# Dilated attention in a two-layer hybrid block: tokens of one residue side by side, heads paired on halves of the array, outputs with features on partitions

## Chip, cores, metric

One core of a Trainium2 chip runs the whole program. The metric is the time of one execution in microseconds, the median of several runs; a profiled execution of its own shows where the time goes. TensorE (PE) multiplies, VectorE (DVE), ScalarE (ACT) and GpSimd (POOL) do the rest, SyncE (SP) issues most DMAs.

## What is computed

512 tokens of width 1024 pass two layers. Each layer has a mixer with three branches (retention, gated delta rule, dilated attention), cross attention to 256 memory tokens, and a convolutional gated MLP, all in float32. The change concerns the third branch and, in the order of its products, the first. Dilated attention, shortened:

```python
DIL_GROUPS = ((128, 1), (512, 4), (2048, 16))     # window, dilation; 4 heads of 64 features each
q, k = partial_rope(d_q), partial_rope(d_k)       # first 16 features of a head are rotated
for gi, (window, dilation) in enumerate(DIL_GROUPS):
    # tokens of one residue modulo dilation form a sequence; blocks of window // dilation,
    # each sees itself and the block before it, at a distance of at most window // dilation
    o_g, lse_g = dilated_window_attention(q[:, :, gi], k[:, :, gi], v[:, :, gi], dilation, window // dilation)
wts = softmax(stack(lses), axis=groups)
o_dil = sum(wts * stack(outs)).reshape(B, T, 256)
merged = gate0 * (o_ret @ w_br_ret) + gate1 * (o_gdn @ w_br_gdn) + gate2 * (o_dil @ w_br_dil)
```

## The kernel before

Activations stand with features on partitions and the 512 tokens along the free axis. Projections are computed from a high and a low part of each operand (fp32r): three matmuls a tile (`mm3`, L214 to L216) into one of four accumulators of PSUM pool `pd`. Weights come in slabs of 512 KB over SP, and ScalarE and VectorE split each into `wh` and `wl` (L203, L204) with the highest priority. The small products of the attention parts are plain fp32; each such call is two load-and-matmul pairs in the trace, a transposition is one.

The code is written as a data flow. A scheduler orders the instructions of every engine ahead of time with a simulated clock: by priority, which is the place in the program unless `soon()` or `first()` raises it, and as operands and buffers are free in that simulation. Engines then run their lists in order. PSUM pools `pa` and `pg` have two buffers each; the scratch tags `ta` three and `tg` four.

`rotated` (L346) multiplies a projection by a cosine row (L349), swaps features (L350), multiplies by sines on POOL (L351) and adds (L352). `mixer` calls it for the twelve tiles `dqk` (three groups; two tiles of queries, two of keys; two heads to a tile, on partitions 0 to 63 and 64 to 127). The projections `dqk` and the values `dv` are on TensorE while `retention` (L595) works through four heads one after another: scores `rs` (L614), state products `rS` (L619), outputs `ro` (L626) and `ri` (L630).

`dilated` (L667) has two halves, i = 0 for group 0 and i = 1 for groups 1 and 2 together. Each has four steps n of 128 queries, and in each step two turns hh, for the heads on the lower and on the upper partitions. A turn writes scores `ds` of two heads (L687; L691, where every 4th token is read by a strided slice), adds the mask, takes the maximum and the exponential, transposes the probabilities (`dt`, L705), copies them to `dp` in SBUF, and multiplies by the values (`do`, L716) with the probabilities stationary and 64 features streaming. The outputs `oA` and `oB` have tokens on partitions. After that the logarithmic sums of the two halves are exchanged through DRAM, the outputs are scaled (L745), transposed (`dA`, `dB`, L750 and L754) and added with a strided view that puts residues back into the order of tokens (L756), and split into `odil` (L757, L758).

`dilated` is followed in the program by `branch` for j = 0, 1, 2. A branch has eight pairs of a gate (24 matmuls) and an output projection `y`; only the third reads `odil`. As the gates and the first two branches need nothing of `dilated`, the scheduler fills TensorE with them while the attention's steps wait for the other engines. The triangular inverse of the second branch uses small tiles of the array: L504 multiplies partitions 0 to 31 into 0 to 31 and 64 to 95 into 64 to 95, L506 partitions 0 to 31 into 32 to 63. After the mixer, four loads of memory tokens use the tag `tg` (L1086, L1087).

Of the kernel before, what the change touches and what calls it, by code (L numbers as in the profile page):

```python
# [12 lines left out]
AF = mybir.ActivationFunctionType  # L13
# [5 lines left out]
P = 128  # L19
# [4 lines left out]
NB = 4  # L24
# [77 lines left out]
def tile_hybrid(ctx, tc, xT, memT, pos, wts, cst, kst, prm, rows, outT):  # L102
# [243 lines left out]
    def rotated(out, p, tab, swap):  # L346
        t = td("rot")
        with soon():
            V.tensor_tensor(out, p, tab[:, 0, :], ALU.mult)  # L349
            V.stream_shuffle(t, p, swap)  # L350
        G.tensor_tensor(t, t, tab[:, 1, :], ALU.mult)  # L351
        V.tensor_tensor(out, out, t, ALU.add)  # L352
# [241 lines left out]

    def retention(l, rqk, rv, dec):  # L595
# [13 lines left out]
        for h in range(H):  # L609
            j, r = h // 2, slice(64 * (h % 2), 64 * (h % 2) + 64)  # L610
            hs = slice(h * P, (h + 1) * P)
            sp = pa(f"rs{h}", (NB, P))
            for b in range(NB):
                PE.matmul(sp[:, b, :], lhsT=rqk[r, 2 + j, blk(b)], rhs=rqk[r, j, blk(b)], start=True, stop=True)  # L614
            st = ta(f"st{h}", (NB, P))
            V.tensor_tensor(st, sp, again(dec[:, h * P:(h + 1) * P], NB), ALU.mult)
            kv = pa(f"rS{h}", (NB - 1, P))
            for b in range(NB - 1):
                PE.matmul(kv[:, b, :], lhsT=ks[j][:, b, :], rhs=rv[:, b, hs], start=True, stop=True)  # L619
            state = states[j][r]  # L620
            S.activation(state[:, 0], kv[r, 0], AF.Copy)
            for b in range(1, NB - 1):
                V.tensor_tensor(state[:, b], state[:, b - 1], kv[r, b], ALU.add)
            op = pg(f"ro{h}", (NB, P))
            for b in range(NB):
                PE.matmul(op[:, b, :], lhsT=st[:, b], rhs=rv[:, b, hs], start=True, stop=True)  # L626
            S.activation(o[:, :, h, :], op, AF.Copy)
            ip = pg(f"ri{h}", (NB - 1, P))
            for b in range(1, NB):
                PE.matmul(ip[:, b - 1, :], lhsT=rqk[r, j, blk(b)], rhs=state[:, b - 1], start=True, stop=True)  # L630
            for b in range(1, NB):
                q = K_QD + 3 * h + b - 1
                V.scalar_tensor_tensor(o[:, b, h, :], ip[:, b - 1], dec[:, q:q + 1], o[:, b, h, :],
                                       ALU.mult, ALU.add)
            sq = ta(f"rsq{h}", (NB, P))
            for b in range(NB):
                i = b * H + h
                S.activation(sq[:, b, :], o[:, b, h, :], AF.Square, accum_out=ssq[:, i:i + 1])
# [28 lines left out]
    def dilated(l, dq, dk, dv0, dv12, kc):  # L667

        oA = region("q1", [NB, H, 64], f"oA{l}")
        oB = region("q2", [NB, H, 64], f"oB{l}")  # L670
        st = [small("stA", 32), small("stB", 32)]
        sd = [dp.tile([T, 8], F32, name=f"sd{l}{i}") for i in range(2)]
        masks = (kc[:, 0:256], kc[:, 256:512])
        for i, o in enumerate((oA, oB)):
            v8 = st[i].rearrange("p (n e) -> p n e", e=8)
            for n in range(NB):
                for hh in range(2):
                    w = P if i == 0 and n == 0 else 2 * P
                    nk = w // P
                    m = masks[i][:, 2 * P - w:]  # L680

                    r, hs = slice(64 * hh, 64 * hh + 64), slice(hh, H, 2)
                    pool = (pa, pg)[hh]
                    sp = pool(f"ds{i}{n}{hh}", (2, 2 * P))[:, :, :w]
                    for hp in range(2):
                        if i == 0:
                            PE.matmul(sp[:, hp, :], lhsT=dq(0, hp)[r, blk(n)],  # L687
                                      rhs=dk(0, hp)[r, (n + 1) * P - w:(n + 1) * P], start=True, stop=True)
                        else:
                            for g in (1, 2):  # L690
                                PE.matmul(sp[:, hp, (g - 1) * P:g * P], lhsT=dq(g, hp)[r, n::NB],  # L691
                                          rhs=dk(g, hp)[r, n::NB], start=True, stop=True)
# [13 lines left out]
                    pt = ta(f"dp{i}{n}{hh}", (2, nk, P))  # L706
                    S.activation(pt, tpz, AF.Copy)
                    op = pool(f"do{i}{n}{hh}", (2, 64))
                    for hp in range(2):
                        h = 2 * hp + hh  # L710
                        for k in range(nk):
                            if i == 0:
                                rhs = dv0[:, n + 1 - nk + k, h * 64:h * 64 + 64]
                            else:
                                rhs = dv12[:, n, k * 256 + h * 64:k * 256 + h * 64 + 64]
                            PE.matmul(op[:, hp, :], lhsT=pt[:, hp, k, :], rhs=rhs,  # L716
                                      start=k == 0, stop=k == nk - 1)
                    S.activation(o[:, n, hs, :], op, AF.Copy)
            if i == 0:
                G.dma_start(sd[0].rearrange("(n p) e -> p n e", p=P), v8)  # L720
            else:
# [555 lines left out]
```

## Time and profile before

| | us |
|---|---|
| median of 3 runs | 2159.71 |
| lowest, highest | 2157.39, 2163.61 |
| the profiled execution | 2165.57 |
| its span, first to last instruction | 2163.7 |
| TensorE busy | 2118.1 |
| VectorE busy | 1374.7 |
| ScalarE busy | 927.5 |
| GpSimd busy | 391.5 |

The page says how long each engine was busy and which chain of work ended last. In the timeline a row is a run of like instructions: start, length, engine, line, operation, tiles and shapes, count. Matmuls overlap, so what one costs is the distance between starts and not its length. In the table by stretch, PEclk is TensorE's granted clock as a share of full speed. The dilated stage and its filler stand at about 355 to 552 us in the first layer and at 1415 to 1612 us in the second.

### The profile page before, as it was taken

The numbers are of one execution on the slowest core, as the hardware profiler recorded it, in microseconds if no ns is written. First come the engines' busy times: TensorE is split into PE (matmuls) and PEld (weight loads), VectorE is DVE, ScalarE is ACT, GpSimd is POOL, SyncE is SP. The second block draws the span as 40 slices with busy tenths as digits, with TensorE's granted clock in tenths as the row PEclk, the third lists the DMA queues.
The fourth block names the chain that finished last, engine by engine and source line by source line (L and its number), as shares of the span: only waits on it lengthen the run. The fifth ranks groups of instructions, "written<-read, shape, count | busy, mean of one in ns | idle before, by whom it ended". The sixth has DMA issues, their size and how long they took to land.

```text
span 2163.7 us, 28806 instructions
## 1 busy us (share of the span) xinstructions
PE 2118.1 (98%) x10665; PEld 1783.8 (82%) x10665; DVE 1374.7 (64%) x2571; ACT 927.5 (43%) x1885; POOL 391.5 (18%) x403
## 2 busy tenths in 40 slices
PE   7899999999999999999999999999999999999997
PEld 6778889888888888888888788988888888888886
DVE  7995585435577786377478846743455788745754
ACT  4733334433455444244356242443343564433443
POOL 6731220002130211011121121100111302100112
PEclk9999999989999999999999999999999999999998
DMA  4233222122233223333332322321333323323322
GB/s 144 78 96 109 84 84 88 60 88 87 94 98 117 78 98 98 98 97 98 111 101 83 110 85 69 93 78 50 98 98 98 108 88 98 98 93 102 98 90 86
DMA packets 69756, 201.58 MB, mean 93 GB/s; under 512 B 18352, under 2 KB 21168, under 8 KB 69104
## 3 DMA queue, kind: packets, MB, share of 16 engines
q1 hardware_dynamic: 67120, 192.34, 28.2%
q0 software_dynamic: 2352, 7.37, 1.1%
q8 instruction: 83, 1.36, 0.3%
q14 instruction: 57, 0.47, 0.1%
q10 hardware_dynamic: 144, 0.04, 0.0%
HBM read 192.85 MB, written 6.88 MB: 92 GB/s over the span
## 4 chain that ended last, share of the span: by engine, by line
PE 86%; DVE 8%; DMA 2%; issue 1%; ACT 1%; SPq 0%; DVEq 0%; ACTq 0%
PE gate L214 4%; PE gate L215 4%; PE gate L216 4%; PE uu L214 3%; PE ua L214 3%; PE uu L215 3%; PE ua L215 3%; PE ua L216 3%; PE uu L216 3%; PE dn L214 3%; PE dn L215 3%; PE dn L216 3%; PE dqk L214 2%; PE dqk L216 2%; PE dqk L215 2%; DVE wl L204 2%
## 5 line engine op out<-in xcount | busy, mean ns | idle before, releaser
L203 ACT ACTIVATE wh<-w 128x512 fp32r<-128x512 f32 (+2 forms) x689 | 429.6, 625 | 852.0 <-PE dn L215 129.4
L204 DVE TENSOR_TENSOR wl<-w,wh 128x512 fp32r<-128x512 f32 (+2 forms) x689 | 507.8, 739 | 381.9 <-ACT wh L203 357.7
L214 PE MATMUL gate<-xgh,wh 128*128 128x512 f32 x384 | 157.3, 410 | 0.0
L215 PE MATMUL gate<-xgl,wh 128*128 128x512 f32 x384 | 155.7, 405 | 0.0
L216 PE MATMUL gate<-xgh,wl 128*128 128x512 f32 x384 | 155.1, 404 | 0.0
L216 PE MATMUL uu<-xgh,wl 128*128 128x512 f32 x320 | 124.6, 389 | 0.0
L214 PE MATMUL uu<-xgh,wh 128*128 128x512 f32 x320 | 124.6, 389 | 0.0
L215 PE MATMUL uu<-xgl,wh 128*128 128x512 f32 x320 | 124.6, 389 | 0.0
L214 PE MATMUL ua<-xgh,wh 128*128 128x512 f32 x320 | 124.6, 389 | 0.0
L216 PE MATMUL ua<-xgh,wl 128*128 128x512 f32 x320 | 124.6, 389 | 0.0
L215 PE MATMUL ua<-xgl,wh 128*128 128x512 f32 x320 | 124.6, 389 | 0.0
L214 PE MATMUL dn<-ah,wh 128*128 128x512 f32 x308 | 120.0, 390 | 0.0
L215 PE MATMUL dn<-al,wh 128*128 128x512 f32 x308 | 120.0, 389 | 0.0
L216 PE MATMUL dn<-ah,wl 128*128 128x512 f32 x308 | 116.2, 389 | 0.0
L1017 POOL TENSOR_TENSOR fya<-fya,fyu 128x512 f32<-128x512 f32 x44 | 72.9, 1657 | 223.1 <-DVE fyu L1001 221.3
L278 POOL TENSOR_TENSOR acc<-acc,sq 128x512 f32<-128x512 f32 x41 | 59.4, 1448 | 244.3 <-ACT sq L277 243.3
L778 POOL TENSOR_TENSOR mg<-mg,g 128x512 f32<-128x512 f32 x32 | 45.8, 1432 | 298.0 <-DVE g L776 298.0
L214 PEld LDWEIGHTS gate<-xgh,wh 128*128 128x128 f32 x384 | 75.4, 196 | 17.6 <-issue 2.6
L216 PEld LDWEIGHTS gate<-xgh,wl 128*128 128x128 f32 x384 | 75.0, 195 | 16.7 <-issue 0.7
L215 PEld LDWEIGHTS gate<-xgl,wh 128*128 128x128 f32 x384 | 75.2, 196 | 15.2 <-issue 0.4
L216 PE MATMUL g<-xgh,wl 128*128 128x512 f32 x192 | 77.6, 405 | 1.5 <-DVE wl L204 1.5
L351 POOL TENSOR_TENSOR rot<-rot,tab 128x512 f32<-128x512 f32 x32 | 47.0, 1478 | 173.7 <-DVE rot L350 164.1
(497 smaller groups left out, 5266.7 us busy)
## 6 DMA issues: line engine op xcount, KB each, us to landing
w<-in_wts SPq DMA_DIRECT2D x331, 512.0 KB, 3.5
tab<-tabs_d POOLq DMA_DIRECT2D x4, 512.0 KB, 4.1
mem<-in_memT POOLq DMA_DIRECT2D x8, 256.0 KB, 3.6
x<-in_xT SPq DMA_DIRECT2D x2, 1024.0 KB, 5.2
x_d<-x SPq DMA_DIRECT2D x8, 256.0 KB, 3.8
x<-x_d SPq DMA_DIRECT2D x2, 1024.0 KB, 5.4
out<-x SPq DMA_DIRECT2D x8, 256.0 KB, 2.3
w<-in_wts SPq DMA_DIRECT2D x7, 256.0 KB, 2.5
```

Of the source, the lines that this page charges most:

```text
L203: S.activation(wh[:, :m], w[:, o:o + m], AF.Copy)
L204: V.tensor_tensor(wl[:, :m], w[:, o:o + m], wh[:, :m], ALU.subtract)
L214: PE.matmul(out, lhsT=lh, rhs=rh, start=start, stop=False)
L215: PE.matmul(out, lhsT=lh, rhs=rl, start=False, stop=False)
L216: PE.matmul(out, lhsT=ll, rhs=rh, start=False, stop=stop)
L278: eng.tensor_tensor(acc, acc, sq, ALU.add)
L351: G.tensor_tensor(t, t, tab[:, 1, :], ALU.mult)
L778: G.tensor_tensor(mt, mt, g, ALU.add)
L1017: G.tensor_tensor(ya, ya, yu, ALU.mult)
```

## The change

Five edits. `rotated` can write its sum so that the tokens of one residue modulo 4 stand side by side; groups 1 and 2 use that, with a scratch tile from `ta`, and their scores then read whole blocks. A helper `together` issues a list of matmuls one right behind the other. In `retention` two heads, and in `dilated` both turns of a step, issue their products alternately on the lower and the upper half of the array's rows. The product with the values is turned round: values stationary, probabilities streaming, the two turns alternately on the left and the right half of the array's columns, so that outputs come with features on partitions. The scale of the outputs is spread over 64 features on POOL and brought to that layout by a product with the identity, and the transpositions `dA` and `dB` go.

```diff
-    def rotated(out, p, tab, swap):
+    def rotated(out, p, tab, swap, every=1):
         t = td("rot")
+        a = out if every == 1 else ta("rota")
         with soon():
-            V.tensor_tensor(out, p, tab[:, 0, :], ALU.mult)
+            V.tensor_tensor(a, p, tab[:, 0, :], ALU.mult)
             V.stream_shuffle(t, p, swap)
         G.tensor_tensor(t, t, tab[:, 1, :], ALU.mult)
-        V.tensor_tensor(out, out, t, ALU.add)
+        if every == 1:
+            V.tensor_tensor(out, a, t, ALU.add)
+        else:
+            a, t = (v.rearrange("p (t n) -> p n t", n=every) for v in (a, t))
+            V.tensor_tensor(out.rearrange("p (n t) -> p n t", n=every), a, t, ALU.add)
...
+    def together(calls):
+        for i, call in enumerate(calls):
+            with (first if i else soon)():
+                ins = call()
+                if i:
+                    tc.keep_in_program_order(ins)
...
     def retention(l, rqk, rv, dec):
...
+        for j in range(2):
+            pair = [(2 * j + e, slice(64 * e, 64 * e + 64)) for e in range(2)]
+            sps = [pa(f"rs{h}", (NB, P)) for h, r in pair]
+            def score(b, e):
+                r = pair[e][1]
+                return PE.matmul(sps[e][:, b, :], lhsT=rqk[r, 2 + j, blk(b)], rhs=rqk[r, j, blk(b)],
+                                 start=True, stop=True)
+            together([lambda a=(b, e): score(*a) for b in range(NB) for e in range(2)])
...
+            ips = [pool(f"ri{h}", (NB - 1, P)) for (h, r), pool in zip(pair, (pg, pa))]
+            def before(b, e):
+                r = pair[e][1]
+                return PE.matmul(ips[e][:, b - 1, :], lhsT=rqk[r, j, blk(b)], rhs=states[j][r][:, b - 1],
+                                 start=True, stop=True)
+            together([lambda a=(b, e): before(*a) for b in range(1, NB) for e in range(2)])
...
     def dilated(l, dq, dk, dv0, dv12, kc):
-        oA = region("q1", [NB, H, 64], f"oA{l}")
-        oB = region("q2", [NB, H, 64], f"oB{l}")
+        oA = region("q1", [2, NB, P], f"oA{l}")
+        oB = region("q2", [2, NB, P], f"oB{l}")
...
+                pools = (pa, pg)
+                sps = [pools[hh](f"ds{i}{n}{hh}", (2, 2 * P))[:, :, :w] for hh in range(2)]
+                def score(hp, g, hh):
+                    keys = slice((n + 1) * P - w, (n + 1) * P) if i == 0 else blk(n)
+                    to = slice(0, w) if i == 0 else blk(g - 1)
+                    return PE.matmul(sps[hh][:, hp, to], lhsT=dq(g, hp)[halves[hh], blk(n)],
+                                     rhs=dk(g, hp)[halves[hh], keys], start=True, stop=True)
+                together([lambda a=(hp, g, hh): score(*a)
+                          for hp in range(2) for g in ((0,), (1, 2))[i] for hh in range(2)])
...
-                                PE.matmul(sp[:, hp, (g - 1) * P:g * P], lhsT=dq(g, hp)[r, n::NB],
-                                          rhs=dk(g, hp)[r, n::NB], start=True, stop=True)
...
-                    pt = ta(f"dp{i}{n}{hh}", (2, nk, P))
-                    S.activation(pt, tpz, AF.Copy)
-                    op = pool(f"do{i}{n}{hh}", (2, 64))
...
-                            PE.matmul(op[:, hp, :], lhsT=pt[:, hp, k, :], rhs=rhs,
-                                      start=k == 0, stop=k == nk - 1)
-                    S.activation(o[:, n, hs, :], op, AF.Copy)
+                    pts.append(tg(f"dp{i}{n}{hh}", (2, nk, P)))
+                    S.activation(pts[hh], tpz, AF.Copy)
+                op = pools[n % 2](f"do{i}{n}", (2, P))
+                def values(hp, k, hh):
...
+                    return PE.matmul(op[halves[hh], hp, :], lhsT=v, rhs=pts[hh][:, hp, k, :],
+                                     start=k == 0, stop=k == nk - 1)
+                together([lambda a=(hp, k, hh): values(*a)
+                          for hp in range(2) for k in range(nk) for hh in range(2)])
+                S.activation(o[:, :, n, :], op, AF.Copy)
...
-            o16 = o.rearrange("p n h d -> p (n h) d")
-            V.tensor_tensor(o16, o16, over(a, 64), ALU.mult)
+            for hp in range(2):
+                wide = ta(f"dw{i}{hp}", (NB, 2, 64))
+                G.tensor_copy(wide, a.rearrange("p (n h o) -> p n h o", h=H, o=1)[:, :, 2 * hp:2 * hp + 2, :]
+                              .to_broadcast([P, NB, 2, 64]))
+                rows = pa(f"dr{i}{hp}", (NB, P))
+                for n in range(NB):
+                    PE.matmul(rows[:, n, :], lhsT=wide[:, n].rearrange("p h d -> p (h d)"), rhs=ident,
+                              start=True, stop=True)
+                V.tensor_tensor(o[:, hp], o[:, hp], rows, ALU.mult)
...
-            transposes(pA, lambda n: oA[:, n, hs, :].rearrange("p h d -> p (h d)"))
...
-            transposes(pB, lambda n: oB[:, n, hs, :].rearrange("p h d -> p (h d)"))
...
-                rotated(dqk[g][:, i, :], fm_one(f"dqk{g}{i}", xg), tab, SWAP8)
+                rotated(dqk[g][:, i, :], fm_one(f"dqk{g}{i}", xg), tab, SWAP8, NB if g else 1)
```

## Rows read from the trace of the kernel before

**Rows 1.** The page: busy time of the engines, and the chain that ended last.
```profile
PE 2118.1 (98%) x10665; PEld 1783.8 (82%) x10665; DVE 1374.7 (64%) x2571; ACT 927.5 (43%) x1885; POOL 391.5 (18%) x403
PE 86%; DVE 8%; DMA 2%; issue 1%; ACT 1%; SPq 0%; DVEq 0%; ACTq 0%
```
**Rows 2.** By stretch: length, busy us (instructions) per engine, PEclk, DMA share, GB/s.
```profile
355.00:420.00 65.00, 65.00 (x317) 52.35 (x315) 30.85 (x55) 28.93 (x72) 0.78 (x1) 1.00 0.22 71
420.00:500.00 80.00, 80.00 (x347) 66.64 (x346) 27.20 (x48) 28.16 (x70) 5.66 (x6) 0.89 0.25 79
1480.00:1560.00 80.00, 80.00 (x350) 66.56 (x349) 27.45 (x51) 27.74 (x70) 4.58 (x4) 0.91 0.24 80
```
**Rows 3.** Groups by line: form and count | busy us, mean ns | idle before.
```profile
L691 PE MATMUL ds<-dqk 64*128 64x128 f32 x128 | 38.7, 446 | 0.0
```
**Rows 4.** Timeline of TensorE, a step of i = 1: start, length, engine, line, form, count.
```profile
475.62 1.00 PE L716 MATMUL do<-dv,dp 128*128 128x64 f32 x8
476.55 2.24 PE L691 MATMUL ds<-dqk 64*128 64x128 f32 x8
478.72 0.72 PE L214 MATMUL gate<-xgh,wh 128*128 128x512 f32 x1
479.23 0.63 PE L215 MATMUL gate<-xgl,wh 128*128 128x512 f32 x1
```
**Rows 5.** Timeline of TensorE, part of a step of i = 0.
```profile
404.92 1.13 PE L687 MATMUL ds<-dqk 64*128 64x256 f32 x4
405.97 0.66 PE L705 MATMUL dt<-c,dm 128*128 128x128 f32 x4
406.39 0.47 PE L215 MATMUL gate<-xgl,wh 128*128 128x512 f32 x1
```
**Rows 6.** Timeline of TensorE, retention: scores alone, state products, then two heads' products meeting.
```profile
296.53 1.16 PE L614 MATMUL rs<-rqk 64*128 64x128 f32 x8
297.61 0.94 PE L619 MATMUL rS<-rv,rk 128*128 128x128 f32 x6
298.30 0.48 PE L216 MATMUL dqk<-xgh,wl 128*128 128x512 f32 x1
...
304.83 0.27 PE L630 MATMUL ri<-rst,rqk 64*128 64x128 f32 x1
304.94 0.27 PE L614 MATMUL rs<-rqk 64*128 64x128 f32 x1
304.94 0.27 PE L630 MATMUL ri<-rst,rqk 64*128 64x128 f32 x1
305.05 0.27 PE L614 MATMUL rs<-rqk 64*128 64x128 f32 x1
```
**Rows 7.** Timeline of TensorE, the triangular inverse: tiles of 32x32, then of 64x64.
```profile
197.92 0.19 PE L506 MATMUL x<-T,ys 32*32 32x32 f32 x1
197.94 0.20 PE L504 MATMUL x<-ys,T 32*32 32x32 f32 x2
197.95 0.19 PE L506 MATMUL x<-T,ys 32*32 32x32 f32 x1
...
202.39 1.14 PE L515 MATMUL y<-A 64*64 64x64 f32 x16
```
**Rows 8.** Additions on VectorE and POOL (ns min/median/max or mean); the rotation's stretch.
```profile
L352 DVE TENSOR_TENSOR dqk<-dqk,rot x24: 676/684/949, 233.2 to 1374.0; 128x512 f32<-128x512 f32 x24
L756 DVE TENSOR_TENSOR dsA<-dsA,dB x4: 1085/1100/1110, 512.7 to 1575.8; 128x512 f32<-128x512 f32 x4
L778 POOL TENSOR_TENSOR mg<-mg,g 128x512 f32<-128x512 f32 x32 | 45.8, 1432 | 298.0 <-DVE g L776 298.0
290.00:310.00 20.00, 20.00 (x112) 16.87 (x111) 19.76 (x55) 4.71 (x11) 6.11 (x4) 1.00 0.27 89
```
**Rows 9.** Timeline: the last write of the output, and its first reader on TensorE.
```profile
519.97 0.69 DVE L758 TENSOR_TENSOR odil<-dsA,odil 128x512 fp32r<-128x512 f32 x1
...
551.30 0.39 PE L214 MATMUL y<-odil,wh 128*128 128x512 f32 x1
```

## What is predicted

> **What bounds the kernel now.** The page first: TensorE is busy 98% of the span, and 86% of the chain of work that ended last is TensorE's [rows 1]. The table by stretch then shows the dilated stage of each layer without a gap: TensorE busy 65.00 of 65 us and 80.00 of 80, vector and scalar engines under half of the time [rows 2]. The gaps between the short matmuls of the attention are filled with gate and branch matmuls that need nothing from it. So a microsecond of TensorE taken out here should come out of the total, as long as such filler lasts. The same table shows the granted clock at 0.89 and 0.91 in the second half of the stage, 1.00 before it [rows 2]. Last comes the order on TensorE, from which I read spacing (start to next start, over the count): a matmul's duration includes its tail.
>
> **Strided scores (groups 1 and 2).** 64 instructions a layer write a product of 128 columns from every 4th token. Eight take 2.17 us (476.55 to 478.72), 0.271 each [rows 4]; the line's busy time gives 38.7/128 = 0.302 [rows 3]. Summing start to start over a layer's twelve groups I get 0.29: 18.6 us. The rotation now writes the tokens side by side, so they become the kind of matmul that retention has. Eight of those, all on one half of the array, take 1.08 us, 0.135 each; where two products on different halves stand together the spacing falls to 0.11 a pair, 0.055 each (304.83, 304.94, 304.94, 305.05) [rows 6]. The change alternates the halves call by call, so I take 0.055: 64 x 0.055 = 3.5, a saving of 15.1 a layer. Bounds: 0.135 (10.0 saved), 0.055.
>
> **Scores of group 0.** Twenty-four of 256 columns at 1.05/4 = 0.262 [rows 5] and eight of 128 at 0.135 [rows 6]: 7.4 us. In pairs 256 columns should take twice 0.11: 24 x 0.11 + 8 x 0.055 = 3.0. Saved 4.4; bounds 0 and 4.4.
>
> **Retention.** 56 instructions a layer on halves of the array. Their 32 groups in both layers, the first at 296.53, sum to 6.0 us a layer, because some pairs meet already [rows 6]. All alternating: 56 x 0.055 = 3.1. Saved 2.9; bounds 0 and, had none met before (56 x 0.135 = 7.6), 4.5.
>
> **Values.** Before, the stationary side is a 128x128 block of probabilities and 64 columns stream; eight take 0.93 us, 0.116 each [rows 4]; 120 a layer make 13.9 us. After, 64 columns of values are stationary, 128 columns stream, and two heads use the left and the right columns of the array. No row shows 128x64 tiles. The nearest is the triangular inverse: tiles of 32x32, of which two read the same rows and write different columns. There a step of one L506 and two L504 takes 0.03 us (197.92 to 197.95), while sixteen instructions of 64 columns on one and the same tile take 1.14 us, 0.07 each, or 0.035 for 32 columns [rows 7]: three instructions in the time of one, so tiles on the same rows do overlap. I take 0.055: 6.6 us, saved 7.3. Bounds: 0.116 (nothing saved) and 0.055.
> The Trainium skill speaks against this: "TensorE: Matmul & The Clock Gate", Part 3 ("What overlaps and what doesn't"), says that a weight load overlaps running matmuls only when the row group differs, and column halves share all row groups. By that page these loads would stand in line; by the rows above they wouldn't. It is a rival below.
>
> **Scaling by rows.** The outputs now have features on partitions, so the softmax weights are widened on POOL and brought to that layout by 32 new full-width instructions a layer; such ones take 0.69/6 = 0.115 [rows 6]: 3.7 us. Sixteen transposes go, at 0.42/4 = 0.105 [rows 5]: 1.7. Net +2.0. The four copies a layer on POOL, priced by its nearest row of the same size at 1.43 us [rows 8], run on an engine that is busy 5.66 of 80 us [rows 2], and wait in its queue only behind the branch additions; they cost nothing while the filler lasts.
>
> **Rotation.** Sixteen additions (eight a layer) now read every 4th element. An addition took 0.684, the nearest strided one 1.100 [rows 8]; +0.42 x 16 = 6.7 us of VectorE, where it is 19.76 of 20 us busy [rows 8]. TensorE doesn't wait there now, and the additions stand behind the two instructions that free the accumulator. The new scratch tile shares three buffers with retention, and VectorE could wait for one. Bounds 0 (a strided read isn't faster) and 6.7; I take 2 in all, because the excess has the following stage's idle VectorE to run into.
>
> **The clock.** After a score group of eight with the values ahead of it (475.62 to 478.72) the following matmuls take 0.63 us instead of 0.39 [rows 4, 9]: the 1.2 GHz level. After the narrower groups of the first half they don't [rows 5], and that half has 1.00 throughout [rows 2]. In both halves the short groups look alike but for the strided scores, so with them the cause should go. (1 - 0.89) x 80 + (1 - 0.91) x 80 = 16.0 us; a part lies under score groups which I have counted already, so 14. Bounds 0 and 16.
>
> **Nothing for the rest.** The probability tiles move to the four "tg" buffers, which pushes the four loads of the memory behind this stage; their readers come after the branches. Fewer, wider copies of outputs, and the products with the keys in one order, change only engines that idle. Switches: a matmul behind a short group lasts some 0.1 longer (0.47 at 406.39, 0.39 elsewhere [rows 5, 9]); fewer groups would give at most 3 us a layer back, which I leave out.
> The Trainium skill's page "TensorEngine Tiling (Array Packing)", Key Properties, says that a change of tiling mode drains the array, and the values bring one mode more. By it some 16 groups x 2 x 0.1 = 3 us would be lost over both layers; no row shows that the mode and not the short group costs the 0.1.
>
> **The sum.** A layer: -15.1 - 4.4 - 2.9 - 7.3 + 2.0 = -27.7; two: -55.4. Clock -14, rotation +2: -67.4. The profiled execution took 2165.57 us: 2098.2. The median of the runs is 5.9 below it, so 2092.
>
> **Rivals.**
> 1. The column halves don't overlap: values stay near 0.116, +7.3 x 2 = 14.6, 2106. For it: no row of this tile shape. Against: [rows 7]. Chance 0.11.
> 2. Their loads stand in line with the streams: 0.11 and half of the 0.115 of a full-width load, 0.168 each, 20.1 us instead of 6.6, +27 in all: 2119. For it: the rule of the Trainium skill named under the values. Against: [rows 7]. Chance 0.04.
> 3. The clock still falls, as the stage keeps many short matmuls: +14, 2106. Against: the first half, as dense in them, holds 1.00 [rows 2]. Chance 0.07.
> 4. The change doesn't do what it says: the calls stand alternately in the program, but the halves don't run together. Scores at 0.135 and 0.262, retention at 0.135, values at 0.116: 5.1 + 4.4 + 4.5 + 7.3 = 21.3 a layer, 2135. Against: the pairs in [rows 6], which met by chance and did. Chance 0.05.
> 5. The other side: TensorE runs out of filler, because the attention's own steps become longer. Its output is ready at 520.7, its first reader starts at 551.3, 30.6 us later [rows 9]. With some 32 us less to do TensorE gets there at about 519. Each layer has 8 steps, of now (520.7 - 355)/8 = 20.7 us. Two score groups of 2.17 become one of 0.9 in four of them, some 14 us off the chain; that is the cushion. But both halves of a step are now tied: scores need a slot in both PSUM pools, values wait for the slower softmax, and in TensorE's queue the filler stands behind them. At 4 us more a step: (32 - 14) x 2 = 36, 2128. Beyond 6 us (8 x 6 - 14 = 34, a layer's whole gain) it is slower; at 7, 2 x 8 over the median: 2176. Against: scalar and vector engines have half their time free [rows 2], and the probabilities get buffers of their own. Chance 0.11, of which 0.04 faster, 0.03 within, 0.04 slower.
>
> **Chances and range.** The forecast has 0.62. Within 0.3% is what a measurement of this kernel can't tell from no change. Faster: 0.62 + 0.11 + 0.04 + 0.07 + 0.05 + 0.04 = 0.93; same 0.03, slower 0.04. The range goes up to 2128, over rivals 1, 2, 3 and the mild part of 5, and leaves out 4 and the bad part of 5. Down: the whole 16 of the clock, no cost of rotation, and the switches (6): 2092 - 2 - 2 - 6 = 2082; retention at its bound 3 more, and the spread of the runs: 2076.
>
> **What would show it.** Right: score instructions spaced 0.055, or 0.11 at 256 columns; values 0.055; granted clock 1.00 through the stage; TensorE still without gaps up to the first reader of the output. Wrong: spacing of 0.11 or more in the values, gate matmuls of 0.63 us, TensorE waiting for probabilities or for the output, VectorE's waits moving into the rotations.

## The result, and the profile after

| | before | after |
|---|---|---|
| median of the runs, us | 2161.20 | 2137.01 (2136.38 to 2139.00) |
| ratio | | 0.9891, 95% interval 0.9874 to 0.9909 |
| profiled execution, span, us | 2163.7 | 2134.6 |
| TensorE busy / idle in the span, us | 2118.1 / 45.6 | 2071.3 / 63.3 |

The change makes the kernel 1.1% faster, by 24 us; the interval of the ratio doesn't reach 1. The forecast was 2092, 69 us less, and 2137 lies outside its range of 2076 to 2128. The page of after, busy time and then the chain that ended last, against [rows 1]:

```profile
PE 2071.3 (97%) x10697; PEld 1738.4 (81%) x10697; DVE 1375.7 (64%) x2575; ACT 921.3 (43%) x1865; POOL 401.3 (19%) x411
PE 83%; DVE 12%; issue 2%; ACT 2%; DMA 1%; SPq 0%; DVEq 0%; ACTq 0%
```

TensorE has 47 us less to do, but it idles 18 us more, and VectorE's share of the chain goes from 8% to 12%. The table by stretch of after says where (length, then busy us and instructions of PE, PEld, DVE, ACT, POOL, then granted clock, DMA share, GB/s):

```profile
275.00:302.00 27.00, 19.47 (x144) 17.47 (x145) 18.64 (x65) 11.00 (x50) 0.92 (x1) 0.87 0.01 2
302.00:345.00 43.00, 39.53 (x225) 33.81 (x223) 38.84 (x79) 14.03 (x32) 13.98 (x10) 0.96 0.30 92
345.00:410.00 65.00, 65.00 (x328) 55.55 (x327) 25.86 (x49) 28.34 (x70) 1.34 (x2) 1.00 0.25 74
410.00:480.00 70.00, 70.00 (x414) 56.44 (x413) 34.68 (x70) 31.98 (x77) 6.84 (x9) 1.00 0.36 118
480.00:535.00 55.00, 55.00 (x261) 46.12 (x260) 30.32 (x51) 20.00 (x38) 11.30 (x11) 1.00 0.33 98
```

The last three rows are the dilated stage, and they answer to [rows 2]: no gap, and the clock at 1.00 where it was 0.89. The loss is in the first two, ahead of that stage, in the rotations and the retention. There TensorE is idle for 11 us of 70, and the clock is down too; in the first row POOL and the DMAs have all but stopped. Before the change, the same two stretches had 0.9 us of idle time and a clock of 1.00:

```profile
275.00:302.00 27.00, 26.08 (x139) 22.02 (x138) 23.42 (x56) 7.86 (x25) 8.36 (x6) 1.00 0.24 78
302.00:345.00 43.00, 43.00 (x293) 40.89 (x293) 33.08 (x93) 19.16 (x59) 6.54 (x8) 1.00 0.35 105
```

The timeline of after across the hole (start, length, engine, line, form, count, idle time and what ended it):

```profile
272.68 0.39 PE L216 MATMUL dqk<-xgh,wl 128*128 128x512 f32 x1
...
279.65 1.62 PE L630 MATMUL rs<-rqk 64*128 64x128 f32 x16 [1.25 <-DVE rk L620]
...
282.03 0.68 DVE L637 TENSOR_TENSOR st<-rs,kc 128x512 f32<-128x512 f32 x1
...
289.50 0.70 PE L655 MATMUL ri<-rst,rqk 64*128 64x128 f32 x5 [2.63 <-DVE rst L645]
...
291.74 2.07 PE L630 MATMUL rs<-rqk 64*128 64x128 f32 x14 [1.42 <-DVE oret L662]
...
298.41 1.06 PE L649 MATMUL ro<-rv,st 128*128 128x128 f32 x8
298.93 0.62 DVE L645 TENSOR_TENSOR rst<-rst,rS 64x128 f32<-64x128 f32 x2 [2.17 <-ACT rst L643]
299.58 0.69 DVE L351 TENSOR_TENSOR rota<-dqk,tab 128x512 f32<-128x512 f32 x1
...
300.99 0.50 PE L214 MATMUL dqk<-xgh,wh 128*128 128x512 f32 x1
301.08 1.30 POOL L353 TENSOR_TENSOR rot<-rot,tab 128x512 f32<-128x512 f32 x1 [51.67 <-DVE rot L352]
```

Between 272.68 and 300.99 TensorE issues no projection of the dilated queries and keys. VectorE's first multiplication into the new scratch tile starts at 299.58, after the last state addition of retention; until then the accumulators of the projections stay full, with four finished projections that nobody takes. In those 28 us TensorE has only the end of the delta rule's scan and retention itself, whose steps wait for VectorE and the scalar engine. The second layer has the same hole: 10.4 us of idle time between 1315 and 1420.

The attention's output is ready at 495.35 and is first read 39.4 us later, against 30.6 in [rows 9]:

```profile
494.67 0.68 DVE L796 TENSOR_TENSOR odil<-oA,odil 128x512 fp32r<-128x512 f32 x1
...
534.74 0.39 PE L214 MATMUL y<-odil,wh 128*128 128x512 f32 x1
```

### The profile page after: what moved, and what is told of

It is laid out like the page before. It is cut to its first block, busy times and chain, and to the rows that moved or that the text cites. A ratio compares the mean times of both kernels' runs of the same rounds, so it can differ in the third digit from the quotient of the medians.

```text
span 2134.6 us, 28839 instructions
## 1 busy us (share of the span) xinstructions
PE 2071.3 (97%) x10697; PEld 1738.4 (81%) x10697; DVE 1375.7 (64%) x2575; ACT 921.3 (43%) x1865; POOL 401.3 (19%) x411
## 4 chain that ended last, share of the span: by engine, by line
PE 83%; DVE 12%; issue 2%; ACT 2%; DMA 1%; SPq 0%; DVEq 0%; ACTq 0%
PE gate L216 4%; PE gate L214 4%; PE gate L215 4%; PE ua L214 3%; PE uu L214 3%; PE uu L216 3%; PE ua L216 3%; PE ua L215 3%; PE uu L215 3%; PE dn L214 3%; PE dn L215 3%; PE dn L216 3%; DVE wl L204 2%; PE y L216 2%; PE y L215 2%
## 5 line engine op out<-in xcount | busy, mean ns | idle before, releaser
L214 PE MATMUL gate<-xgh,wh 128*128 128x512 f32 x384 | 151.3, 394 | 0.0
L215 PE MATMUL gate<-xgl,wh 128*128 128x512 f32 x384 | 150.0, 391 | 0.0
L353 POOL TENSOR_TENSOR rot<-rot,tab 128x512 f32<-128x512 f32 x32 | 53.1, 1658 | 214.4 <-DVE rot L352 197.9
L215 PEld LDWEIGHTS gate<-xgl,wh 128*128 128x128 f32 x384 | 72.2, 188 | 14.7
```

Of the source, the lines that this page charges most:

```text
L214: PE.matmul(out, lhsT=lh, rhs=rh, start=start, stop=False)
L215: PE.matmul(out, lhsT=lh, rhs=rl, start=False, stop=False)
```

## The experiments

Theory A: the scratch tile `rota` is taken from the tag `ta`, whose three buffers go out in program order. Retention takes eight tiles of that tag and stands ahead of these rotations in the program, so all rotations of groups 1 and 2 are held until retention is nearly through. Theory B: the hole is retention's own, because its heads now go in pairs and wait for each other. Beside this, each term of the sum was to be measured by itself. The kernel before had a median of 2158.31 us beside the first four kernels below (up to layout_alone), 2163.62 beside strided_pairs, the two kernels by halves and layout_scores, and 2162.27 beside the last four, so kernels are compared by their ratios to it; where a step is small, also by the span and TensorE's busy time of the profiled runs, which are single executions. The counts and prices of small products below are of the trace's instructions, two to a call.

**rota_cv: the scratch tile from another tag, of four buffers.**

```diff
-        a = out if every == 1 else ta("rota")
+        a = out if every == 1 else cv("rota")
```

> The changed kernel with one word different: the scratch tile of the rotation comes from the tag cv, which nothing uses at that time, instead of ta, which retention uses. Theory A (buffers of a tag go out in the order of the program, so the rotations of groups 1 and 2 wait in ta behind retention's tiles, the four accumulators stay full and TensorE has no filler between 273 and 301 us): the projections run on through retention, TensorE's idle time of 11 us and the low clock of some 4 us a layer go, about 2107 us. Theory B (retention in pairs starves TensorE, whatever the tag): 2137, with the same hole. Theory C (VectorE is too full there with strided additions): about 2125, the hole shorter, waits of TensorE for VectorE.

Measured 2113.16 us, ratio 0.9785 (0.9770 to 0.9799): 1.06% of 2160, 23 us, come back with one word. Of the 22.9 us between the spans (2134.6 and 2111.7), 13.1 are idle time of TensorE and 9.8 busy time; the lower clock in the two stretches of after accounts for about that much of the latter (27 x 0.13 + 43 x 0.04 = 5 us in the first layer, and the second is alike). Its table by stretch:

```profile
275.00:302.00 27.00, 27.00 (x151) 22.91 (x150) 21.60 (x42) 8.12 (x25) 4.56 (x3) 1.00 0.25 77
302.00:345.00 43.00, 40.67 (x271) 39.13 (x271) 31.48 (x93) 16.62 (x55) 4.00 (x4) 1.00 0.27 81
```

The first stretch is full again, where after had 19.47 of 27. In the second, 2.33 us of idle time stay, in one piece of its timeline:

```profile
312.83 0.72 DVE L352 STREAM_SHUFFLE rot<-dqk 128x512 f32<-128x512 f32 x1
...
313.61 0.38 PE L214 MATMUL dv<-wh,xgh 128*128 128x256 f32 x1 [2.33 <-DVE rot L352]
```

A projection waits for the accumulator that VectorE's shuffle frees, so VectorE is the late one here: 2113 is 6 us above theory A's 2107, and part of what theory C expected is there.

That the buffers of `ta` were merely full, and not owed to earlier requests, can be read off the timeline of after. The only other user of the tag up to there in the first layer, the rotation tables, has its last tile sent off at 117 us, and retention writes its first tile of it, `st`, at 282.03. So for 9 us after 272.68 all three buffers lay empty, and `rota` was not written. It was written 0.1 us after the products that read the last `st` (298.41, until 299.47): retention's sixth tile of the tag, three ahead of the first `rota`, the ninth.

**old_retention: retention head by head as before, `rota` still from `ta`.** The paired loop of `retention` is replaced by the one before.

> The changed kernel with retention head by head as before; rotations still take their scratch from ta. Theory A: the hole stays, as retention's tiles are as many and come first; 2135 to 2145 us. Theory B: the hole goes, about 2110 us.

Measured 2139.56 us, ratio 0.9909 (0.9887 to 0.9931): no faster than after. The hole is still in its table by stretch, with the DMAs at a stand:

```profile
275.00:302.00 27.00, 23.34 (x140) 21.30 (x140) 19.23 (x65) 10.29 (x47) 1.47 (x2) 0.75 0.00 1
```

Theory B falls; the hole does not need the pairs.

**rota_cv_old_retention: both edits.**

> Both: scratch from cv and retention head by head. Beside the run with cv alone it prices the pairs in retention: by the rows of before 2.9 us a layer, so 6 us slower than that run, about 2113 us by theory A. Theory B: as fast as or faster than the run with cv alone.

Measured 2114.67 us, ratio 0.9792 (0.9775 to 0.9808). The pairs in retention are worth 3.8 us of TensorE's busy time (2065.3 against 2061.5) and 1.3 us of span, where 6 us were expected: too little for the runs to tell.

**layout_alone: the kernel before with the tokens written in order of use, and nothing else.**

```diff
-                            PE.matmul(sp[:, hp, (g - 1) * P:g * P], lhsT=dq(g, hp)[r, n::NB],
-                                      rhs=dk(g, hp)[r, n::NB], start=True, stop=True)
+                            PE.matmul(sp[:, hp, (g - 1) * P:g * P], lhsT=dq(g, hp)[r, blk(n)],
+                                      rhs=dk(g, hp)[r, blk(n)], start=True, stop=True)
```

(and `rotated` as in the change, its scratch tile from `cv`)

> The kernel before with the tokens of one residue side by side and nothing else (scratch from cv): scores of groups 1 and 2 read whole blocks, one head after the other, values and scaling as before. Theory: scores at 0.135 instead of 0.29 us give 10 us a layer, and the granted clock of 1.00 through the stage gives 14: 2161 - 34 = 2127 us. Rival (the clock falls because of dense short matmuls, not because of the strided reads): 2141, with the clock at 0.9 in the second half of the stage.

Measured 2132.30 us, ratio 0.9874 (0.9860 to 0.9889), span 2131.4. The layout alone, with its tile in `cv`, gives as much as the whole change did with its tile in `ta` (0.9891; the intervals overlap). The group by line (form and count, busy us, mean ns, idle before):

```profile
L697 PE MATMUL ds<-dqk 64*128 64x128 f32 x128 | 20.6, 291 | 0.0
```

The second half of the stage, by stretch:

```profile
440.00:540.00 100.00, 100.00 (x495) 83.28 (x494) 53.68 (x96) 41.98 (x90) 15.69 (x12) 1.00 0.32 104
```

And a step of i = 1 on TensorE:

```profile
459.93 1.00 PE L722 MATMUL do<-dv,dp 128*128 128x64 f32 x8
460.87 1.16 PE L697 MATMUL ds<-dqk 64*128 64x128 f32 x8
461.95 0.50 PE L214 MATMUL gate<-xgh,wh 128*128 128x512 f32 x1
462.29 0.39 PE L215 MATMUL gate<-xgl,wh 128*128 128x512 f32 x1
```

Busy 20.6 where [rows 3] has 38.7; eight scores in 1.08 us (460.87 to 461.95) where [rows 4] has 2.17; and the matmuls behind them take 0.50 and then 0.39, at a clock of 1.00.

**strided_pairs: the whole change except the layout.**

```diff
-                    keys = slice((n + 1) * P - w, (n + 1) * P) if i == 0 else blk(n)
+                    mine, keys = (blk(n), slice((n + 1) * P - w, (n + 1) * P)) if i == 0 else (slice(n, None, NB),) * 2
...
```

(the queries are read by `mine`, and `rotated` adds in place as before, without a scratch tile)

> The changed kernel without its layout part: groups 1 and 2 rotated in place as before, scores of i=1 read every fourth token, but on alternate row halves. Theory (the layout itself removes the cost of the strided read, about 0.14 us of 0.29 per product, and with it the stretch at a lower clock): the spacing of these products stays near 0.15 us as pairs, 64 x 0.08 = 5 us a layer over the contiguous pairs, granted clock again below 0.95 in the second half of the stage; with about 2 us a layer saved on VectorE: 2120 to 2135 us. Rival (the alternation alone hides the strided read, since the halves load beside each other): spacing 0.07, clock 1.00, 2109 to 2114 us.

Measured 2121.00 us, ratio 0.9806 (0.9792 to 0.9821), inside the theory's 2120 to 2135. A step of i = 1 on TensorE:

```profile
459.31 1.09 PE L750 MATMUL do<-dp,dv 128*64 128x128 f32 x16
460.33 2.24 PE L717 MATMUL ds<-dqk 64*128 64x128 f32 x14
462.50 0.50 PE L215 MATMUL gate<-xgl,wh 128*128 128x512 f32 x1
```

The second half of the stage, by stretch:

```profile
420.00:500.00 80.00, 80.00 (x432) 64.52 (x431) 38.82 (x71) 31.82 (x76) 12.68 (x14) 1.00 0.35 112
```

Two things come out. Fourteen strided score instructions, eight on one half of the rows and six on the other, take 2.17 us, what eight on one half took in [rows 4]: alternation hides one half behind the other, strided or not, but it doesn't remove the stride's price. And the clock stays at 1.00 with the strided reads still there, so that part of the expectation missed: the strided reads are not enough by themselves to bring it down. Against rota_cv TensorE is busy 15.2 us more (2076.7 against 2061.5) and idle 5.2 us less (45.0 against 50.2): in these two profiles the contiguous products gain three times what VectorE's strided additions cost. By the ratios the net is 4.5 us and not 10, with intervals that overlap.

**scores_by_half: scores not alternately, all of one row half first.**

```diff
-                          for hp in range(2) for g in ((0,), (1, 2))[i] for hh in range(2)])
+                          for hh in range(2) for hp in range(2) for g in ((0,), (1, 2))[i]])
```

> The changed kernel with the rotation's scratch tiles under `cv`, and the paired score products of the dilated stage issued all of the first row half, then all of the second. Theory (the row halves overlap when they alternate): start-to-start of a 128-wide score goes from 0.068 to about 0.135 us and of a 256-wide one from 0.133 to about 0.26 us: 64 x 0.067 + 28 x 0.13 = 8 us a layer, so about 2129 us. Rival (the order of issue does not matter, only the contiguous layout does): 2113 us within 3, the same spacings as now.

(`rota` from `cv`, as in all kernels from here on)

Measured 2122.32 us, ratio 0.9811 (0.9796 to 0.9826): 5.6 us more than rota_cv by the ratios, TensorE busy 11.0 us more. Its timeline of TensorE:

```profile
413.85 1.16 PE L717 MATMUL ds<-dqk 64*128 64x128 f32 x8
414.93 1.09 PE L750 MATMUL do<-dp,dv 128*64 128x128 f32 x16
415.95 1.16 PE L717 MATMUL ds<-dqk 64*128 64x128 f32 x8
```

And that of rota_cv:

```profile
408.41 1.13 PE L717 MATMUL ds<-dqk 64*128 64x256 f32 x8
409.47 0.50 PE L215 MATMUL gate<-xgl,wh 128*128 128x512 f32 x1
...
440.46 1.09 PE L750 MATMUL do<-dp,dv 128*64 128x128 f32 x16
441.49 1.16 PE L717 MATMUL ds<-dqk 64*128 64x128 f32 x16
442.58 0.50 PE L216 MATMUL gate<-xgh,wl 128*128 128x512 f32 x1
...
451.76 0.48 PE L717 MATMUL ds<-dqk 64*128 64x128 f32 x2
...
457.67 1.09 PE L750 MATMUL do<-dp,dv 128*64 128x128 f32 x16
458.70 1.16 PE L717 MATMUL ds<-dqk 64*128 64x128 f32 x14
```

Eight on one half last as long as sixteen alternately: 0.135 each (413.85 to 414.93) against 0.068 (441.49 to 442.58). The rival falls, the row halves do run together. The gain of alternating is below the expected 16 us because rota_cv doesn't alternate perfectly. The x2 at 451.76 is a first score product issued 7 us ahead of its group: alone, as `together` holds only the later calls in order. Its group of fourteen at 458.70 then lasts no less than sixteen, since eight of it are on one half.

**values_by_half: the same for the values, whose halves are columns.**

```diff
-                          for hp in range(2) for k in range(nk) for hh in range(2)])
+                          for hh in range(2) for hp in range(2) for k in range(nk)])
```

> The changed kernel with the rotation's scratch tiles under `cv`, and the values products issued all of the first half of the columns, then all of the second, instead of alternately. Theory (products on the two column halves of the array overlap only when their neighbours are on the other half): start-to-start of a values product goes from 0.064 us in groups of 16 to about 0.12 us, some 220 products a layer, so about +12 us a layer at most and +7 at least: 2125 to 2137 us. Rival (column halves don't overlap, the gain over the kernel before is only the smaller width of the product): the spacing stays 0.064 and the time stays 2113 us within 3.

Measured 2123.89 us, ratio 0.9816 (0.9800 to 0.9832): 6.7 us more than rota_cv by the ratios, TensorE busy 10.0 us more, 5 a layer. That is under the 7 to 12 expected, which counted some 220 value products a layer; the trace has 120 instructions. Its timeline of TensorE:

```profile
425.85 1.09 PE L750 MATMUL do<-dp,dv 128*64 128x128 f32 x8
...
427.30 1.09 PE L750 MATMUL do<-dp,dv 128*64 128x128 f32 x8
428.31 1.16 PE L717 MATMUL ds<-dqk 64*128 64x128 f32 x14
```

Eight on one column half take what sixteen take alternately (427.30 to 428.31, 0.126 each, against 440.46 to 441.49, 0.064 each). Products on the two column halves, which read the same rows, do run side by side, with their loads: in rota_cv's group the loads, 0.137 us long each, start in pairs, one for each half, within 0.01 us of each other.

**layout_scores: layout and paired scores; values, scaling and retention as before.** The loops of these three parts are those of the kernel before, but the values of both turns now follow the softmax of both, with their probabilities in `tg`.

> The kernel before with two parts of the change: groups 1 and 2 written in order of use (scratch tiles under `cv`), and the dilated scores on alternate row halves; values, scaling and retention are those of before. The layout alone took 2132.3 us; everything but the pairs in retention took 2114.7. Theory (scores by pairs and values by pairs are each worth their products' spacing): scores 64 x 0.067 + 28 x 0.13 = 8 us a layer, less group edges, so 2118 to 2122 us, and the values with the new scaling another 2 to 4 us a layer. Rival (pairs of scores gain nothing because the row halves overlapped only within a strided read): 2132 us, and all of the rest is the values.

Measured 2118.69 us, ratio 0.9797 (0.9783 to 0.9812), span 2120.3: 11.1 us of span under layout_alone, 16.6 by the ratios, about what the theory said. To rota_cv_old_retention, which adds the values and the scaling, there are 7.3 us of span and 7.8 of busy time, but only 0.0005 of the ratio, 1 us; the runs don't settle which. Start to start, the values sum to 14.7 us a layer here and to 13.6 in layout_alone, so this kernel pays 1.1 a layer for its new order, and as a step between the two it shows the scores too small and the values too large by that much.

**late_half_first: the half whose data come last goes first, so that no product runs ahead of its group.**

```diff
-                          for hp in range(2) for k in range(nk) for hh in range(2)])
+                          for hp in range(2) for k in range(nk) for hh in (1, 0)])
```

(and the same in the scores)

> The changed kernel with the rotation's scratch tiles under `cv`, and in the dilated scores and values the half whose data come last (heads 1 and 3) issued first, so that the first product of a group, the only one not held in program order, waits for the same thing as the rest. Theory (the shortfall of the paired products against 0.055 us each is the group edge, about 0.2 us, paid twice where the first product runs ahead alone: 10 to 12 such lone pairs a layer): 2 to 4 us a layer less, ratio to the version with only `cv` 0.996 to 0.998, and the groups of 14 become groups of 16. Rival (the lone product costs nothing, since a group's edge is drained behind filler work anyway): no difference within 0.1%.

Measured 2114.59 us, ratio 0.9781 (0.9760 to 0.9802): no difference to 0.9785, as the rival said. The values then stand in whole groups, but of the scores some still run ahead, as at 447.86 in the timeline:

```profile
437.82 1.16 PE L717 MATMUL ds<-dqk 64*128 64x128 f32 x16
...
447.86 0.49 PE L717 MATMUL ds<-dqk 64*128 64x128 f32 x2
```

For the values I sum, start to start, 7.8 us a layer instead of 8.8 in rota_cv; the scores take 0.4 more, and the 1 us that this leaves over both layers is too small to show in the time.

**strided_writes, additions_in_order, late_half_writes: the rotation's addition.**

```diff
-            a, t = (v.rearrange("p (t n) -> p n t", n=every) for v in (a, t))
-            V.tensor_tensor(out.rearrange("p (n t) -> p n t", n=every), a, t, ALU.add)
+            a, t = (v.rearrange("p (t n) -> p t n", n=every) for v in (a, t))
+            V.tensor_tensor(out.rearrange("p (n t) -> p t n", n=every), a, t, ALU.add)
```

(strided_writes; additions_in_order adds with all three operands in order, so it leaves out the new order of the tokens and serves as a price only; late_half_writes is this edit with late_half_first)

> The changed kernel with the scratch tiles under `cv`, and the rotation's addition reads its two inputs in order and writes its output to every 512th byte, where the changed kernel reads both at a stride of four elements and writes in order. Theory (it is the strided read that takes 1.05 to 1.07 us against 0.684 us for the same addition in order): 0.684 us each again, 16 x 0.37 = 5.9 us of VectorE over both layers, of which up to 4.7 us of TensorE's idle time in the rotation comes back: ratio 0.998 to the version with only `cv`. Rival (any stride on any operand costs the same): 1.05 us, no difference.

> The changed kernel with the scratch tiles under `cv` and the rotation's additions of groups 1 and 2 with all three operands in order: the tokens are then not side by side by their order of use, and the attention of these groups sees other neighbours than the reference's; the number and shape of all instructions are the same. It prices the strided additions: 0.684 us against 1.05 to 1.07, 16 of them. Theory (TensorE's 2.3 us of idle time a layer in the rotation is these): 3 to 5 us less than with `cv` alone, and 300 to 345 us filled as before the change. Rival (the idle time comes from the wait for GpSimd's multiplication, which the scratch tile does not shorten): no difference.

> The two foregoing edits that keep the result, together with `cv`: late half first, and the rotation's addition reading in order and writing at a stride. If both are worth what their theories say, 4 to 9 us less than `cv` alone, ratio to the kernel before 0.974 to 0.977; if neither is, 0.9785.

Measured: 2111.90 us (0.9773, 0.9751 to 0.9795), 2106.64 (0.9742, 0.9722 to 0.9762) and 2110.97 (0.9765, 0.9743 to 0.9786). The addition in rota_cv, strided_writes and additions_in_order (ns, min/median/max):

```profile
L358 DVE TENSOR_TENSOR dqk<-rota,rot x16: 1058/1075/1618, 284.5 to 1347.1; 128x512 f32<-128x512 f32 x16
```
```profile
L358 DVE TENSOR_TENSOR dqk<-rota,rot x16: 1052/1096/1612, 283.9 to 1347.3; 128x512 f32<-128x512 f32 x16
```
```profile
L358 DVE TENSOR_TENSOR dqk<-rota,rot x16: 674/684/1186, 282.3 to 1339.7; 128x512 f32<-128x512 f32 x16
```

The stretch of rota_cv's idle 2.33 us, in additions_in_order:

```profile
300.00:345.00 45.00, 45.00 (x295) 43.63 (x294) 30.22 (x89) 18.45 (x59) 3.65 (x4) 1.00 0.30 89
```

A stride on the output costs what two on the inputs cost, as the rival of strided_writes said. With none, the rotation's idle time is gone in both layers, 2.3 us each; of the 7.6 us of idle time that additions_in_order has less than rota_cv, the other 3 lie before 255 us, where nothing was edited. So this cost is 5 us of the 9 that the ratios show. Of the versions that compute the same as the kernel before, late_half_writes has the lowest median and rota_cv the least edit; their intervals overlap, and both beat both kernels. Its 0.9765 lies in the range that its expectation gave for both edits, but its interval (0.9743 to 0.9786) reaches to the 0.9785 that it gave for neither, and neither edit showed a gain by itself.

## Why the prediction was wrong

The steps, each by the span of the profiled runs against the span before, and by the ratios of all runs times 2160 (us, both layers). The two differ by up to 6 us a step: a span is one execution, the runs of one kernel spread over 1 to 12 us, and the profiled execution of before was slower than the runs beside it (2165.57 against 2157 to 2164). A ratio's interval is about 3 us to either side, so a step by ratios is good to 4 or 5 us.

| step | forecast | by span | by ratio | between |
|---|---|---|---|---|
| layout: strided read, clock, rotation | -32 | -32.3 | -27 | before, layout_alone |
| alternate scores, groups 0 to 2 | -19 | -11.1 | -16.6 | layout_alone, layout_scores |
| values and scaling | -10.6 | -7.3 | -1.1 | layout_scores, rota_cv_old_retention |
| retention in pairs | -5.8 | -1.3 | -1.5 | rota_cv_old_retention, rota_cv |
| scratch tile from `ta` | 0 (in the +2 of the rotation) | +22.9 | +22.9 | rota_cv, after |
| sum | -67.4 | -29.1 | -23.5 | before, after |

(The forecast's strided scores are split here at 0.135: 64 x (0.29 - 0.135) x 2 = 19.9 for the layout, with the clock's 14 and the rotation's +2; the rest goes to the second line. The second and third lines belong together: -18.4 by the spans, -17.7 by the ratios. Summed start to start in layout_alone and rota_cv_old_retention, the scores give 17.3 - 10.5 = 6.8 us a layer, values and scaling 13.6 - 9.2 - 2.0 = 2.4.)

- **The step that failed** is in the rotation: "The new scratch tile shares three buffers with retention, and VectorE could wait for one. Bounds 0 (a strided read isn't faster) and 6.7; I take 2 in all". I named the shared buffers and then priced them by the length of the additions. What comes with a shared tag is an order: the tile waits its turn behind those asked for earlier in the program, here retention's, and the accumulators, POOL and TensorE's filler wait with it. It cost 23 us, 11 a layer, and it alone puts the result outside the range: 2137 - 23 = 2114 lies within. Of the rest, the 22 us from 2092 to 2114, about 15 are the ends of groups and products that run ahead (the points on scores, values and retention). The prediction had named the sign, VectorE's waits moving into the rotations, but gave it no price. That 2137 is close to the 2135 of rival 4 is chance: its mechanism, halves that don't run together, is refuted by the two kernels by halves.
- **Filler.** "As long as such filler lasts" was asked for the dilated stage alone, where it held: no gap there in after, and a margin of 39 us at the output. That the projections in the rotation's stretch are retention's filler, and that the change could take them away, stands nowhere in the text. Rival 5 had the right sentence, in the wrong stage.
- **Score spacing.** The 0.055 was right inside a group, but a group also has two ends, and the forecast left them out. Narrow windows on rota_cv's group of sixteen cut its row into its second and third pair and its last pair:

```profile
441.70 0.39 PE L717 MATMUL ds<-dqk 64*128 64x128 f32 x4
...
442.37 0.28 PE L717 MATMUL ds<-dqk 64*128 64x128 f32 x2
```

From the second pair to the eighth it is 0.67 us, 0.11 a pair, 0.056 each. From the first start (441.49) to the second pair, and from the last pair to the next matmul (442.58), it is 0.21 each. So a group costs some 0.2 us more than its pace, and the average is 0.068, and 0.133 for 256 columns (408.41 to 409.47). The four instructions of [rows 6] met inside a group and show no end, while the 0.135 of the single group there contains its own. Start to start, the scores of a layer sum to 10.3 us in rota_cv (9.6 in after) instead of 6.5. Of the 3.8, 72 x 0.068 + 24 x 0.133 - 6.5 = 1.6 are the ends, and the rest the products that run ahead.
- **Values**: the mechanism was right, 0.064 in whole groups against 0.055, again the ends; 8.8 us a layer in rota_cv (8.5 in after) instead of 6.6, and 7.8 in late_half_first, where the groups are whole. Rival 1, that column halves don't overlap, is refuted by values_by_half. So is rival 2: "TensorE: Matmul & The Clock Gate", Part 3, of the Trainium skill says that a load overlaps running matmuls only where the row group differs. Here the row groups are the same and the pair runs in the time of one, 0.064 each against 0.126, and not at the 0.168 that its rule would give. The measurement decides.
- **Scaling** by rows, +2.0 a layer: the new products sum to 3.4 us a layer against 3.7. The POOL copies took 0.612 us each in after where I priced 1.43; TensorE has no gap in that stretch, so they cost nothing, as said.
- **The clock** came back as forecast, 1.00 through the stage. Over all runs on record the mean granted clock is 0.987 to 0.992 before and 0.995 to 0.997 in layout_alone; from 0.990 and 0.996 I estimate 2160 x 0.010 - 2132 x 0.004 = 13 us, near the 14. The reason given, the strided scores alone, was too simple: strided_pairs keeps the strided reads and also has 1.00. What decides stays open. In the hole of after the clock is down to 0.87, where TensorE idles.
- **Retention**: -1.3 of span and -3.8 of busy time for -5.8. Start to start, its paired products sum to 4.3 us in the first layer of rota_cv and 5.0 in the second, against 5.7 in rota_cv_old_retention and the 3.1 forecast: the same ends and lone products. The time is too small to be settled here.
- **Rotation itself**: 1.07 us an addition as priced (0.684 + 0.42 = 1.10), and 4.7 us of idle time in rota_cv, inside the bounds 0 and 6.7. "TensorE doesn't wait there now" was true of the 20 us of [rows 8], and with VectorE 19.76 of them busy it was also a warning; just ahead of them TensorE had waited 0.48 us for a rotation's shuffle already before the change:

```profile
282.25 0.50 PE L214 MATMUL dqk<-xgh,wh 128*128 128x512 f32 x1 [0.48 <-DVE rot L350]
```

- **Mode changes**: the Trainium skill's page "TensorEngine Tiling (Array Packing)", Key Properties, says that a change of tiling mode drains the array. A wide matmul lasts 0.50 behind a group on half the rows (461.95 in layout_alone), but already 0.48 behind six full-width products, where the mode doesn't change [rows 6], and 0.39 elsewhere. So of the 0.1 that I put on the mode at the end of a group, about 0.02 can be its own; what entering a mode costs, no run here separates.

## What to carry to other kernels

When a change asks for a buffer, look up its tag, who asks for the same tag earlier in the program, and when those let go: the request stands behind them even while the buffers lie empty, and the work that used to fill the waits of the earlier stage stands behind the request. Write an array in the order in which the matrix products read it, even where the write costs VectorE a strided pass (5 us here for 15, by the profiles), and alternate small products between halves of the array, by rows or by columns, each group whole. Price a group of small products by its pace inside (0.055 us a product in pairs here) plus its two ends (some 0.2 us), and count the groups, with the products that run ahead of theirs.

## What the runs showed of the hardware

- A matmul instruction of 128 columns with operands at a stride of 16 bytes took 0.271 us, contiguous 0.135 (eight in 2.17 and 1.08). An addition of 512 elements on VectorE took 1.07 with both inputs at that stride, 1.10 with the output at 512 bytes and 0.684 in order. The Trainium skill's page "SBUF — State Buffer", under "Door 1: The DMA port swizzle", says that each access which moves on to another 16-byte line pays; a stride of four fp32 elements does so at every element, and both rows agree; the sizes are these runs' own.
- Two products on the left and the right columns of the array, reading the same rows, overlap together with their weight loads: 0.064 us each alternately, 0.126 on one half. Inside a group a pair, on halves of the rows or of the columns, takes 0.11 us; a group's ends add some 0.2 us.
- One product issued ahead of a group of alternating ones takes a slot of its own (the x2 rows, 0.48 us with the end) and saves the group nothing: fourteen left of sixteen last the same 1.16 us.
